# A decoder trunk in one program: the order of the attention's sigmoids, and where two pairs' products stand among the projections

## The chip, the cores and the metric

The kernel runs on one core of one Trainium2 chip. The metric is the device time of one execution in microseconds (us); below it is the median of three runs. A profile of one execution gives the start and the duration of every instruction on each engine: PE does the matmuls (PEld is its loading of weights), ACT and DVE the elementwise work, POOL small sums, and SP issues the transfers.

## The reference, cut to what matters

Two layers, each followed by a squared-ReLU MLP, over 512 tokens of width 1024. The first layer mixes by pooling, the second by stick-breaking attention with 16 heads of 64 channels. The change lies in the attention alone.

```python
def stick_breaking_attention(q, k, v):
    ...
    for i in range(S // Q_BLOCK):
        kv_len = (i + 1) * Q_BLOCK
        ...
        z = jnp.einsum('bhqd,bhkd->bhqk', q_blk, k_blk,
                       preferred_element_type=jnp.float32) * inv_sqrt_d
        ...
        log1m = jnp.where(mask, -jax.nn.softplus(z), 0.0)
        excl = lax.cumsum(log1m, axis=3, reverse=True) - log1m
        a = jnp.where(mask, jnp.exp(jax.nn.log_sigmoid(z) + excl), 0.0)
        outs.append(jnp.einsum('bhqk,bhkd->bhqd', a, v_blk.astype(jnp.float32)))
```

So a weight is sigmoid(z) times the product of the 1 - sigmoid(z) = sigmoid(-z) of all later keys before the query. The values are mixed with these weights, and the result goes through the output projection `w_o`.

## The kernel before, in words

Every fp32 operand of a matmul is split in two: a high half, cast by ACT (`nc.scalar.copy`), and the residual, subtracted by DVE. A product is then three matmuls: high by high, high by residual, residual by high. PSUM has eight tiles of 128x512, taken in turn as they come free (`ps()`).

The attention works on eight pairs of heads. `ATT_ORDER` is a written list of its steps, and PE's instructions stand in exactly that order; ACT, DVE and SP are ordered by a scheduler, except that ACT keeps the written order inside `weights`. A step is a letter, the pair, and digits:

- K: the first slices of a pair's key projection (`start`). A projection has eight slices of three matmuls of 128x512; K22 does two slices for pair 2.
- P: the rest of the key projection, then the query projection (`queries_keys`, `project`). ACT casts kh and qh (L967), DVE subtracts kl and ql (L968). Behind each of the two a `fill()` asks for the next weights.
- S: the scores of both heads (`scores`, L1084) into six PSUM tiles, three per head, then `weights`. ACT computes per head four negative sigmoids u (`against`, L1007, the factors 1 - sigmoid) and three positive ones w (`for_`, L1019). A PSUM tile of scores is free once its positive sigmoid is done. DVE runs a scan over u (L1023, tile e) and multiplies w by it (`weigh`, L1029). There is one e, so the second head's scan follows the first head's multiplication.
- T: PE transposes the w of both heads (`turn`, L1042) into six PSUM tiles; ACT casts ah (L1048) and DVE subtracts al (L1052), which frees the tile.
- A: the products of a pair with the values (`products`, L1059), one PSUM tile per head; ACT copies a half of it to o (L1066), DVE adds the other half (L1070). The pair's output o is split into two halves, both called ohl (ACT L292, DVE L293), which the output projection O reads (L311 to L313).

The steps of one pair are spread over three rounds: while S works on pair p, A works on pair p - 1. In the second and the third round a copy (ACT L170) and a residual (DVE L172) of a weight of the output projection are made as well.

Of the kernel before, what the change touches and what calls it, by code (L numbers as in the profile page):

```python
# [15 lines left out]
P = 128  # L16
# [41 lines left out]

ATT_ORDER = [
    (w[0], int(w[1]), [int(c) for c in w[2:]])  # L60
    for w in """H001 N2 H101 N3 H023 H123 P0 K12 S0 P1 T0 K22 S1 A0 P2 T1 K32 S2 A1 P3 O001 T2 O023 S3 A2 P4 V20 T3 V21
    S4 A3 P5 V22 T4 V23 S5 A4 P6 V30 T5 V31 S6 A5 V323 P7 T6 E1""".split()
]

# [41 lines left out]
def trunk(ctx, tc, x, consts, grow, pw, wup, wdn, wq, wk, wv, wo, out):  # L106
# [68 lines left out]
    def gains(lo, n):  # L175


        def scaled(raw):
            m = max(n, 4)
            for k in range(m):  # L180
                c, at = raw[:, k * D // m : (k + 1) * D // m], lo + k * n // m
                nc.scalar.mul(c, c, gc[:, at : at + 1])  # L182

        return scaled
# [3 lines left out]
    def want(key, src, scaled=None):  # L188
        queue.append((key, src, scaled))
# [57 lines left out]
    def fill(n=1):  # L247
        if gate[0]:
            behind.update(latest)
        for _ in range(n):  # L250
            if queue and len(made) < ahead and (queue[0][0][0] != "dn" or dn_pool[0]):
                make()
# [6 lines left out]
    for l in range(2):  # L259
        if l == 1:  # L260
            n = len(queue)
            for what, i, part in ATT_ORDER:
                if what == "H" and not i and 0 in part:
                    for h in range(4):
                        want(("v", 0, h), wv[h], gains(C_KV * KC + 2 * h, 2))
                elif what == "V" and 0 in part:
                    for h in range(2):
                        want(("v", i, h), wv[2 * i + h], gains(C_KV * KC + 4 * h, 4))
                elif what == "K":
                    want(("k", i), wk[i], gains(C_KV * KC, KC))  # L270
                elif what == "P":
                    if ("k", i) not in [k for k, _, _ in queue]:
                        want(("k", i), wk[i], gains(C_KV * KC, KC))
                    want(("q", i), wq[i], gains(C_MIX_PRE1 * KC, KC))
                elif what == "O" and 0 in part or what == "E":
                    for c in range(2 * i, 2 * i + 2 if what == "O" else PAIRS):
                        want(("o", c), wo[c])
            apart.extend(x for x in queue[n:] if x[0] not in [("o", c) for c in range(2)])
            at = [k for k, _, _ in apart].index(("v", 0, 2))
            later = [apart.pop(at) for _ in range(2)]  # L280
            at = [k for k, _, _ in apart].index(("q", 1)) + 1
            apart[at:at] = later

            queue[n - GRP : n + GRP] = queue[n : n + GRP] + queue[n - GRP : n]
        for j in range(NJ):
            want(("up", l, j), wup[l, j])
        for j in range(NJ - GRP, NJ):
            want(("dn", l, j), wdn[l, j])
# [153 lines left out]
    def need(*tiles):  # L442
        for t in tiles:
            if t in pending:
                pending.pop(t).transpose()
# [444 lines left out]
    with tc.tile_pool(name="att", bufs=1, reuse_waits="tile") as ap:  # L890
# [14 lines left out]
        def half_values(i, part):  # L905


            if not half_w:
                half_w.extend(get(("v", 0, h)) for h in range(4))
                for u in range(2):  # L910
                    vs[u] = None, value_tile(u)
            for s in part:
                if i == 0:
                    half_bank[s] = ps()
                for k in range(4 * i, 4 * i + 4):
                    (wh, wl), c = half_w[k // 2], NS[k % 2]
                    mm3(
                        half_bank[s], xnh[:, k, TS[s]], xnl[:, k, TS[s]], wh[:, c], wl[:, c], k == 0, k == KC - 1
                    )
                if i == 1:  # L920
                    for u in range(2):
                        value_parts(vs[u][1], s, half_bank[s][:, u * 256 : u * 256 + 256])
            if i == 1 and T - 1 in part:
                fill(ahead)

        def values(u, part):
            if u not in vs:
                vs[u] = [get(("v", u, h)) for h in range(2)], value_tile(u)
            w, v = vs[u]
            for s in part:  # L930
                pv = ps()
                for k in range(KC):
                    c = slice((k % 4) * 256, (k % 4) * 256 + 256)
                    mm3(
                        pv[:, :256], xnh[:, k, TS[s]], xnl[:, k, TS[s]],
                        w[k // 4][0][:, c], w[k // 4][1][:, c], k == 0, k == KC - 1,
                    )
                value_parts(v, s, pv[:, :256])
# [3 lines left out]
        def start(key, n):  # L942

            started[key] = ps(), get(key), n
            up_block(*started[key][:2], slice(0, S), ks=range(n))

        def project(key):
            if key in started:
                pq, w, n = started.pop(key)
                up_block(pq, w, slice(0, S), ks=range(n, KC))  # L950
            else:
                pq = ps()
                up_block(pq, get(key), slice(0, S))
            return pq

        def qk_tile(tag):
            return ap.tile([P, S], F32R, tag=tag, name=name(tag))
# [1 line left out]
        half = [slice(0, HD), slice(HD, P)]  # L959


        def queries_keys(p):
            both = []
            for what in "kq":
                src = project((what, p))
                hi, lo = qk_tile(f"{what}h"), qk_tile(f"{what}l")
                latest["act"] = nc.scalar.copy(hi, src)  # L967
                latest["dve"] = nc.vector.tensor_tensor(out=lo, in0=src, in1=hi.bitcast(F32), op=ALU.subtract)  # L968
                both.append((hi, lo))
                fill()  # L970
            return both

        begin = ap.tile([P, NSEG], mybir.dt.bfloat16, tag="begin", name="begin")
        us = [ap.tile([P, NSEG + 1], F32, tag=f"u{a}", name=f"u{a}") for a in range(2)]
# [97 lines left out]
        def scores(hs, b):  # L1072


            (kh, kl), (qh, ql) = hs[0].qk
            for x in hs:
                x.pz[b] = ps()
            o = 0
            for i in Head.SCORES[b][0]:
                n = SEG[i][1]  # L1080
                for m, (x, y) in enumerate(((qh, kh), (qh, kl), (ql, kh))):
                    for h in hs:
                        own = half[h.a]
                        nc.tensor.matmul(  # L1084
                            h.pz[b][:, o : o + n], x[own, TS[i]], y[own, :n], start=m == 0, stop=m == 2,
                        )
                o += n

        def weights(p):
            hs = [Head(qk[p], p, a) for a in range(2)]  # L1090
            for b in range(3):
                scores(hs, b)
            with tc.manual_schedule(engines={mybir.EngineType.Activation}):
                for x in hs:
                    for b in range(3):
                        x.against(b)
                hs[0].scan()
                for x in hs:
                    for b in range(3):
                        x.for_(b)  # L1100
            hs[0].weigh()
            hs[1].scan()
            hs[1].weigh()
            return hs

        def transposed(hs):
# [146 lines left out]
        def until(key):  # L1253
            while key not in made:
                make()

        qk, heads, gpost1 = {}, {}, None

        def step(what, i, part):
            nonlocal gpost1  # L1260
            if what == "H":
                half_values(i, part)
            elif what == "V":
                values(i, part)
            elif what == "N":
                need(i)
            elif what == "K":
                start(("k", i), *part)
            elif what == "P":
                qk[i] = queries_keys(i)  # L1270
                if i == PAIRS - 1:
                    until(("o", 5))
            elif what == "S":
                gate[0] = True
                heads[i] = weights(i)
                fill()
            elif what == "T":
                transposed([heads[i][a] for a in part or range(2)])
                behind.update(latest)
            elif what == "A":  # L1280
                mix_pair(i, vs[i // 2][1])
            elif what == "O" and part:
                out_proj(i, part)
                if gpost1 is None:
                    with tc.issue_after(latest["sp"].ins):
                        gpost1 = gain_row(R_MIX_POST1)
# [66 lines left out]
```

## Time and profile before

| | us |
|---|---|
| median of 3 runs | 950.59 (949.9 to 950.76) |
| profiled execution | 950.39 |
| its span | 948.6 |
| first to last step of interest: S1 to the first output projection | 419.50 to 455.16 |

A row of the page's busy times gives an engine's busy us, its share of the span and its instructions. A row of waits reads: engine, tile and line, then what it waited for, with us in total, times, and the longest. A row of windows gives a stretch in us from the span's start, its length, then the busy us of PE, PEld, DVE, ACT and POOL (with the count of instructions), the clock that PE was granted, the share of the transfer engines and GB/s. A row of the timeline gives the start, the duration, engine, line and operation, out<-in, and in brackets the idle time before it and who ended it; x6 means that six such instructions are drawn together.

### The profile page before, as it was taken

What the parts mean: (1) busy time and instruction counts of PE and PEld (TensorE: products, weight loads), DVE (VectorE), ACT (ScalarE), POOL (GpSimd) and SP (SyncE); (2) the same over time, 40 slices, a digit from 0 to 9 for tenths busy, and PEclk for the clock granted to TensorE, in tenths of its full rate; (3) what the DMA queues carried; (4) which work ended last, traced back from release to release, by engine and by line L of the source; (5) the groups of instructions that cost most, each with busy time, mean ns of one, the idle gap of its engine ahead of it and who ended that gap; (6) DMA issues with size and microseconds to landing.
All of it is one profiled execution on the core that took longest, in us unless ns stands there. A gap on an engine that the chain in (4) does not pass through costs nothing.

```text
span 948.6 us, 12348 instructions
## 1 busy us (share of the span) xinstructions
PE 937.6 (99%) x4702; PEld 789.9 (83%) x4702; DVE 696.4 (73%) x797; ACT 560.4 (59%) x983; POOL 41.1 (4%) x83
## 2 busy tenths in 40 slices
PE   9999999999999999999999999999999999999996
PEld 7998888888888888887888988898888888888885
DVE  5865798988978976178466668884696966958756
ACT  6667979788775646165544444875645444444532
POOL 2300000000000004000000000200000000000002
PEclk9999999999999999999999999999999999999999
DMA  8244969789697860630434271342514243133102
GB/s 309 95 181 140 348 218 346 293 284 353 216 326 264 298 195 2 222 133 1 170 119 171 97 267 45 134 156 74 193 45 133 89 133 111 45 133 112 37 7 90
DMA packets 43262, 156.15 MB, mean 165 GB/s; under 512 B 4289, under 2 KB 4673, under 8 KB 43202
## 3 DMA queue, kind: packets, MB, share of 16 engines
q1 hardware_dynamic: 43202, 155.36, 46.7%
q8 instruction: 37, 0.61, 0.3%
q14 instruction: 23, 0.19, 0.1%
HBM read 121.79 MB, written 33.55 MB: 164 GB/s over the span
## 4 chain that ended last, share of the span: by engine, by line
PE 96%; ACT 1%; DVE 1%; POOL 1%; issue 0%; POOLq 0%; DVEq 0%; ACTq 0%
PE ps L600 28%; PE ps L722 15%; PE ps L719 15%; PE ps L723 15%; PE ps L311 4%; PE ps L312 4%; PE ps L313 4%; PE ps L1059 2%; PE ps L1042 2%; PE ps L1084 2%; PE ps L840 1%; PE ps L406 1%; PE ps L812 1%; PE ps L767 1%; ACT xn L296 1%; ACT u L1007 0%
## 5 line engine op out<-in xcount | busy, mean ns | idle before, releaser
L600 PE MATMUL ps<-w,a 128*128 128x512 f32 x1176 | 278.6, 389 | 0.0
L722 PE MATMUL ps<-xnh,w 128*128 128x512 f32 (+1 forms) x704 | 260.2, 371 | 0.0
L723 PE MATMUL ps<-xnl,w 128*128 128x512 f32 (+1 forms) x704 | 259.7, 370 | 0.0
L719 PE MATMUL ps<-xnh,w 128*128 128x512 f32 (+1 forms) x704 | 259.1, 370 | 0.1
L600 PEld LDWEIGHTS ps<-w,a 128*128 128x128 f32 x1176 | 220.7, 188 | 45.9 <-DVE w L293 0.2
L719 PEld LDWEIGHTS ps<-xnh,w 128*128 128x128 f32 x704 | 132.1, 188 | 22.9 <-DVE w L861 0.3
L723 PEld LDWEIGHTS ps<-xnl,w 128*128 128x128 f32 x704 | 132.7, 188 | 22.1
L722 PEld LDWEIGHTS ps<-xnh,w 128*128 128x128 f32 x704 | 132.2, 188 | 22.3
L609 DVE TENSOR_TENSOR y<-ps,y 128x512 f32<-128x512 f32 x124 | 84.3, 686 | 43.8 <-PE ps L600 43.7
L172 DVE TENSOR_TENSOR w<-raw,w 128x1024 fp32r<-128x1024 f32 x58 | 70.9, 1222 | 57.2 <-ACT w L170 57.1
L170 ACT CAST w<-raw 128x1024 fp32r<-128x1024 f32 x58 | 61.0, 1051 | 80.3 <-PE ps L719 80.3
L292 ACT CAST a<-r 128x768 fp32r<-128x768 f32 (+1 forms) x60 | 47.6, 794 | 72.0 <-PE ps L600 55.4
L293 DVE TENSOR_TENSOR a<-r,a 128x768 fp32r<-128x768 f32 (+1 forms) x60 | 54.0, 900 | 11.8 <-ACT a L292 11.6
L1023 DVE TENSOR_TENSOR_SCAN e<-u,begin 128x1280 f32<-128x1280 f32 x16 | 45.2, 2825 | 18.6 <-ACT u L1007 18.3
L292 ACT CAST w<-e 128x1536 fp32r<-128x1536 f32 (+1 forms) x30 | 41.9, 1395 | 23.3 <-DVE e L574 13.9
L293 DVE TENSOR_TENSOR w<-e,w 128x1536 fp32r<-128x1536 f32 (+1 forms) x30 | 49.4, 1647 | 1.8 <-ACT w L292 1.6
L182 ACT ACTIVATE apart<-apart,eye 128x128 f32<-128x128 f32 (+1 forms) x132 | 43.1, 407 | 0.3 <-DMA apart<-in_wk 0.3
L293 DVE TENSOR_TENSOR w<-w,w 128x1536 fp32r<-128x1536 f32 (+1 forms) x20 | 33.0, 1649 | 8.4 <-ACT w L292 8.4
L632 ACT ACTIVATE r<-ps 128x512 f32<-128x512 f32 x56 | 33.0, 590 | 8.8 <-PE ps L719 8.7
L293 DVE TENSOR_TENSOR w<-xn,w 128x1536 fp32r<-128x1536 f32 (+1 forms) x20 | 33.0, 1650 | 5.6 <-ACT w L292 5.5
L633 ACT ACTIVATE r<-r 128x512 f32<-128x512 f32 x56 | 35.5, 634 | 1.3
L296 ACT ACTIVATE xn<-y 128x512 f32<-128x512 f32 (+1 forms) x25 | 15.3, 613 | 32.2 <-DVE y L478 28.6
(134 smaller groups left out, 1327.6 us busy)
## 6 DMA issues: line engine op xcount, KB each, us to landing
raw<-in_wup SPq DMA_DIRECT2D x64, 512.0 KB, 4.1
w<-kept SPq DMA_DIRECT2D x60, 512.0 KB, 4.3
kept<-wx SPq DMA_DIRECT2D x30, 512.0 KB, 4.7
w<-in_wdn SPq DMA_DIRECT2D x8, 1536.0 KB, 6.7
kept<-apart SPq DMA_DIRECT2D x24, 512.0 KB, 6.0
xn<-in_wdn SPq DMA_DIRECT2D x8, 1536.0 KB, 7.6
apart<-in_wk SPq DMA_DIRECT2D x7, 512.0 KB, 7.5
apart<-in_wq SPq DMA_DIRECT2D x7, 512.0 KB, 9.3
```

The costliest lines, as they stand in the source:

```text
L170: nc.scalar.copy(hi, raw)
L172: nc.vector.tensor_tensor(out=lo, in0=raw, in1=hi.bitcast(F32), op=ALU.subtract)
L182: nc.scalar.mul(c, c, gc[:, at : at + 1])
L292: latest["act"] = nc.scalar.copy(hi, src)
L293: latest["dve"] = nc.vector.tensor_tensor(out=lo, in0=src, in1=hi.bitcast(F32), op=ALU.subtract)
L311: nc.tensor.matmul(dst, ah, bh, start=start, stop=False)
L600: nc.tensor.matmul(bank, a[:, x, q, TS[t]], w[:, z, q], start=start and q == 0 and k == 0, stop=q == self.n - 1 and k == 2, skip_group_che ...
L609: nc.vector.tensor_tensor(out=part, in0=bank, in1=part, op=ALU.add)
L719: nc.tensor.matmul(pu[:, cols], wl[:, k, :], xnh[:, k, cols], start=False, stop=k == KC - 1)
L722: nc.tensor.matmul(pu[:, cols], wh[:, k, :], xnh[:, k, cols], start=k == 0, stop=False)
L723: nc.tensor.matmul(pu[:, cols], wh[:, k, :], xnl[:, k, cols], start=False, stop=False)
L1023: nc.vector.tensor_tensor_scan(out=self.e[:, ::-1], data0=self.u[:, 1:][:, ::-1], data1=begin[:, ::-1], initial=0.0, op0=ALU.mult, op1=ALU ...
```

## The change

`weights` computes the sigmoids of one head completely, negative and positive, followed by its scan and its multiplication, and then those of the other head. The pairs P2 and P3 are cut in two steps, J for the keys and Q for the queries, and the products of the pair before (A0, A1) stand between them instead of ahead of both. K2 and K3 start three slices instead of two.

```diff
 ATT_ORDER = [
-    for w in """H001 N2 H101 N3 H023 H123 P0 K12 S0 P1 T0 K22 S1 A0 P2 T1 K32 S2 A1 P3 O001 T2 O023 S3 A2 P4 V20 T3 V21
+    for w in """H001 N2 H101 N3 H023 H123 P0 K12 S0 P1 T0 K23 S1 J2 A0 Q2 T1 K33 S2 J3 A1 Q3 O001 T2 O023 S3 A2 P4 V20 T3 V21
...
-        def queries_keys(p):
-            both = []
-            for what in "kq":
+        def queries_keys(p, which="kq"):
+            for what in which:
...
-                both.append((hi, lo))
+                qk.setdefault(p, []).append((hi, lo))
                 fill()
-            return both
...
                 for x in hs:
                     for b in range(3):
                         x.against(b)
-                hs[0].scan()
-                for x in hs:
                     for b in range(3):
                         x.for_(b)
-            hs[0].weigh()
-            hs[1].scan()
-            hs[1].weigh()
+                    x.scan()
+                    x.weigh()
...
-            elif what == "P":
-                qk[i] = queries_keys(i)
+            elif what in "PJQ":
+                queries_keys(i, {"P": "kq", "J": "k", "Q": "q"}[what])
```

PE in the second round, at the end of the scores S1 (the tile ps431 holds the last scores, ps439 the first product, ps425 the keys of pair 2). Before:

```order
L1084 MATMUL ps431_3591<-kh401_3481,ql405_3511 128x128
L1059 MATMUL ps439_3635<-ah408_3518,v367_3176 128x512
L1059 MATMUL ps439_3635<-al409_3519,v367_3176 128x512
L1059 MATMUL ps439_3635<-ah411_3527,v367_3176 128x384
L1059 MATMUL ps439_3635<-al412_3528,v367_3176 128x384
```

Now:

```order
L1082 MATMUL ps431_3594<-kh401_3481,ql405_3511 128x128
L722 MATMUL ps425_3567<-xnh_80,w384_3363 128x512
L723 MATMUL ps425_3567<-xnl_81,w384_3363 128x512
L719 MATMUL ps425_3567<-xnh_80,w384_3363 128x512
L722 MATMUL ps425_3567<-xnh_80,w384_3363 128x512
```

The 16 matmuls of the products follow after 15 matmuls of the keys, and 24 of the queries come behind them; the third round is changed in the same way.

ACT in the same round (u1 is head 1's negative sigmoids, w433 and w432 head 0's positive ones, w434 head 1's, o the pair's output, ohl its high half, w436 a weight of the output projection, kh the keys of pair 2). Before:

```order
L1007 ACTIVATE u1_3146<-ps431_3591 128x127
L1019 ACTIVATE w433_3616<-ps426_3574 128x512
L1019 ACTIVATE w433_3616<-ps428_3582 128x384
L1019 ACTIVATE w433_3616<-ps430_3590 128x384
L1019 ACTIVATE w434_3620<-ps427_3575 128x512
L1019 ACTIVATE w434_3620<-ps429_3583 128x384
L1019 ACTIVATE w434_3620<-ps431_3591 128x384
L1066 COPY o438_3634<-ps439_3635 64x512
L1066 COPY o438_3634<-ps440_3646 64x512
L292 CAST ohl441_3657<-o438_3634 128x512
L170 CAST w436_3629<-raw437_3630 128x1024
L967 CAST kh442_3678<-ps425_3567 128x512
```

Now:

```order
L1005 ACTIVATE u1_3146<-ps427_3578 128x511
L1005 ACTIVATE u1_3146<-ps429_3586 128x383
L1005 ACTIVATE u1_3146<-ps431_3594 128x255
L1005 ACTIVATE u1_3146<-ps431_3594 128x127
L1017 ACTIVATE w434_3624<-ps427_3578 128x512
L1017 ACTIVATE w434_3624<-ps429_3586 128x384
L1017 ACTIVATE w434_3624<-ps431_3594 128x384
L170 CAST w436_3632<-raw437_3633 128x1024
L966 CAST kh438_3652<-ps425_3567 128x512
L1064 COPY o440_3656<-ps441_3657 64x512
L1064 COPY o440_3656<-ps442_3668 64x512
L292 CAST ohl443_3679<-o440_3656 128x512
```

Head 0's three positive sigmoids have moved ahead of head 1's negative ones, and the weight's copy and kh have moved ahead of the output's copies and its cast; behind the cast stand, as before it, the queries' cast, a second weight's copy and the six casts of the transposes.

DVE in the same round. Before:

```order
L1029 TENSOR_TENSOR w433_3616<-w433_3616,e432_3614 128x1280
L1023 SCALAR_TENSOR_TENSOR e435_3626<-u1_3146,begin_3144 128x1280
L1070 TENSOR_TENSOR o438_3634<-ps439_3635,o438_3634 64x512
L1070 TENSOR_TENSOR o438_3634<-ps440_3646,o438_3634 64x512
L1029 TENSOR_TENSOR w434_3620<-w434_3620,e435_3626 128x1280
L293 TENSOR_TENSOR ohl441_3657<-o438_3634,ohl441_3657 128x512
L172 TENSOR_TENSOR w436_3629<-raw437_3630,w436_3629 128x1024
L968 TENSOR_TENSOR kl443_3679<-ps425_3567,kh442_3678 128x512
L968 TENSOR_TENSOR ql446_3708<-ps444_3682,qh445_3707 128x512
L172 TENSOR_TENSOR w447_3711<-raw448_3712,w447_3711 128x1024
L1052 TENSOR_TENSOR al451_3718<-ps449_3716,ah450_3717 128x512
```

Now:

```order
L1027 TENSOR_TENSOR w432_3613<-w432_3613,e433_3617 128x1280
L1021 SCALAR_TENSOR_TENSOR e435_3628<-u1_3146,begin_3144 128x1280
L172 TENSOR_TENSOR w436_3632<-raw437_3633,w436_3632 128x1024
L1027 TENSOR_TENSOR w434_3624<-w434_3624,e435_3628 128x1280
L967 TENSOR_TENSOR kl439_3653<-ps425_3567,kh438_3652 128x512
L1068 TENSOR_TENSOR o440_3656<-ps441_3657,o440_3656 64x512
L1068 TENSOR_TENSOR o440_3656<-ps442_3668,o440_3656 64x512
L293 TENSOR_TENSOR ohl443_3679<-o440_3656,ohl443_3679 128x512
L967 TENSOR_TENSOR ql446_3708<-ps444_3682,qh445_3707 128x512
L172 TENSOR_TENSOR w447_3711<-raw448_3712,w447_3711 128x1024
L1050 TENSOR_TENSOR al451_3718<-ps449_3716,ah450_3717 128x512
```

The weight's residual and kl have moved ahead of the two adds of o, and the multiplication of head 1 stands ahead of them too; the residual of the output is the neighbour of ql now.

More of the change, by code (lines that the diff above doesn't have):

```diff
@@ L270, in trunk @@
                     want(("k", i), wk[i], gains(C_KV * KC, KC))
-                elif what == "P":
+                elif what in "PQ":
                     if ("k", i) not in [k for k, _, _ in queue]:
@@ L1268, in step @@
                 start(("k", i), *part)
-            elif what == "P":
-                qk[i] = queries_keys(i)
+            elif what in "PJQ":
+                queries_keys(i, {"P": "kq", "J": "k", "Q": "q"}[what])
                 if i == PAIRS - 1:
```

## The prediction

> **What bounds the kernel now.** I read the page first: its span, its busy times and the shares of the chain that ended last.
>
> ```profile
> span 948.6 us, 12348 instructions
> PE 937.6 (99%) x4702; PEld 789.9 (83%) x4702; DVE 696.4 (73%) x797; ACT 560.4 (59%) x983; POOL 41.1 (4%) x83
> PE 96%; ACT 1%; DVE 1%; POOL 1%; issue 0%; POOLq 0%; DVEq 0%; ACTq 0%
> ```
>
> PE sets the end. The change adds and removes no matmul, so only PE's waits can be won or lost. This execution took 950.39 us, 1.8 more than its span; the median of the three runs, 950.59, lies 0.20 above it. What a measurement of this kernel can tell from no change is about 0.2%, 1.9 us.
>
> The list of PE's waits comes next, and then the windows of PE's steps: the scores of S1, S2 and S3, the products of A0, A1 and A2, and the projections P2 and P3.
>
> ```profile
> PE ps L1059 <- ACT w L1019: 2.1, 2, 1.1
> PE ps L1084 <- DVE al L1052: 0.2, 1, 0.2
> ```
>
> ```profile
> 419.50:421.56 2.06, 2.06 (x25) 1.88 (x24) 0.90 (x2) 1.07 (x2) 0.00 (x0) 1.00 0.27 103
> 438.75:441.74 2.99, 2.77 (x26) 2.15 (x25) 2.43 (x5) 1.70 (x4) 0.00 (x0) 1.00 0.00 0
> 468.64:470.71 2.07, 2.07 (x26) 1.87 (x25) 0.00 (x0) 1.60 (x3) 0.00 (x0) 1.00 0.79 247
> 421.56:425.45 3.89, 2.81 (x18) 2.49 (x17) 3.04 (x2) 3.73 (x11) 0.00 (x0) 1.00 0.00 1
> 441.74:445.55 3.81, 2.84 (x18) 2.50 (x17) 3.06 (x2) 3.75 (x11) 0.00 (x0) 1.00 0.00 0
> 470.71:473.30 2.59, 2.59 (x19) 2.42 (x17) 1.84 (x1) 2.44 (x9) 0.00 (x0) 1.00 0.94 373
> 425.45:435.08 9.63, 9.63 (x45) 7.90 (x44) 9.19 (x8) 3.98 (x7) 0.00 (x0) 1.00 0.00 0
> 445.55:455.16 9.61, 9.61 (x44) 7.93 (x44) 8.03 (x7) 3.00 (x6) 0.00 (x0) 1.00 0.30 110
> ```
>
> The first figure of a row is the stretch. Products without a wait take 2.59 (A2), so A0 loses 1.30 and A1 1.22. Scores take 2.07 (S3), so S2 loses 0.92. That is 3.44 in all, and it bounds the gain here. P2 and P3 hold 42 matmuls each, 0.229 apiece. The granted clock is 1.00 everywhere.
>
> By the idle of the wait list the same three losses are 2.3. [...] With the idle alone the sum below would come to 1.3 instead of 1.8. I go by the stretches.
>
> ```profile
> 424.13 0.50 PE L1059 MATMUL ps<-ah,v 128*128 128x512 f32 x1 [1.08 <-ACT w L1019]
> 444.21 0.50 PE L1059 MATMUL ps<-ah,v 128*128 128x512 f32 x1 [0.97 <-ACT w L1019]
> 440.90 0.38 PE L1084 MATMUL ps<-kh,qh 64*128 64x256 f32 x1 [0.22 <-DVE al L1052]
> 438.42 0.40 PE L719 MATMUL ps<-xnh,w 128*128 128x512 f32 x1
> 438.75 0.53 PE L1084 MATMUL ps<-kh,qh 64*128 64x512 f32 x2
> ```
>
> The kernel has eight PSUM banks. In A0 and A1 six hold scores, one the half-done key projection, one the first head's product; the second product (424.13, 444.21) waits until ACT's first positive sigmoid frees a score bank. In S2 the scores wait for banks that DVE's residuals (al) of the transposes free.
>
> ```profile
> 420.49 1.07 ACT L1007 ACTIVATE u<-ps 128x511 f32<-128x511 f32 x2 [1.36 <-PE ps L1084]
> 421.72 1.87 ACT L1007 ACTIVATE u<-ps 128x255 f32<-128x255 f32 x6 [0.16 <-PE ps L1084]
> 423.42 2.68 ACT L1019 ACTIVATE w<-ps 128x512 f32<-128x512 f32 x6
> 426.13 1.19 ACT L1066 COPY o<-ps 64x512 f32<-64x512 f32 x2
> 430.90 0.62 ACT L292 CAST ohl<-o 128x512 fp32r<-128x512 f32 x1 [3.59 <-DVE o L1070]
> 431.43 1.05 ACT L170 CAST w<-raw 128x1024 fp32r<-128x1024 f32 x1
> 432.50 0.59 ACT L967 CAST kh<-ps 128x512 fp32r<-128x512 f32 x1
> 435.33 0.59 ACT L967 CAST qh<-ps 128x512 fp32r<-128x512 f32 x1 [2.24 <-PE ps L719]
> 435.81 1.05 ACT L170 CAST w<-raw 128x1024 fp32r<-128x1024 f32 x1
> 436.76 2.60 ACT L1048 CAST ah<-ps 128x512 fp32r<-128x512 f32 x6
> ```
>
> ```profile
> 422.31 2.82 DVE L1023 TENSOR_TENSOR_SCAN e<-u,begin 128x1280 f32<-128x1280 f32 x1 [1.91 <-ACT u L1007]
> 425.23 1.49 DVE L1029 TENSOR_TENSOR w<-w,e 128x1280 f32<-128x1280 f32 x1
> 426.76 2.82 DVE L1023 TENSOR_TENSOR_SCAN e<-u,begin 128x1280 f32<-128x1280 f32 x1
> 429.50 1.37 DVE L1070 TENSOR_TENSOR o<-ps,o 64x512 f32<-64x512 f32 x2
> 430.90 1.49 DVE L1029 TENSOR_TENSOR w<-w,e 128x1280 f32<-128x1280 f32 x1
> 432.31 0.68 DVE L293 TENSOR_TENSOR ohl<-o,ohl 128x512 fp32r<-128x512 f32 x1
> 432.91 1.22 DVE L172 TENSOR_TENSOR w<-raw,w 128x1024 fp32r<-128x1024 f32 x1
> 434.05 0.68 DVE L968 TENSOR_TENSOR kl<-ps,kh 128x512 fp32r<-128x512 f32 x1
> 435.95 0.69 DVE L968 TENSOR_TENSOR ql<-ps,qh 128x512 fp32r<-128x512 f32 x1 [1.22 <-ACT qh L967]
> 436.90 1.23 DVE L172 TENSOR_TENSOR w<-raw,w 128x1024 fp32r<-128x1024 f32 x1 [0.25 <-ACT w L170]
> 438.04 3.14 DVE L1052 TENSOR_TENSOR al<-ps,ah 128x512 fp32r<-128x512 f32 x6
> ```
>
> These are ACT's and DVE's queues for the second step. From 422.31 to the end of the residuals at 441.18 DVE stands still for some 1.5 us only; this chain decides when S2 gets its banks.
>
> **The sigmoids, head by head.** The same 14 per pair, in another order. The first positive one now follows head 0's four negative ones, which end just before the scan at 422.31; from its start to the product that it frees are 424.13 - 423.42 = 0.71. With nothing else changed the bank would be free at about 423.0, and the second product asks for it at 421.56 + 1.30 = 422.86: the wait would be nearly gone by this alone. The two parts of the change cure the same wait and do not add. Head 1's negative sigmoids come three positive ones later (2.68 / 6 = 0.45 each, 1.35), ready at 421.72 + 1.87 + 1.35 = 424.9, before the second scan at 426.76; that slack of 1.8 is the cover, beyond it each us would be a us of DVE's chain. The other pairs showed no such wait, so I cost the order there at nothing.
>
> **The products moved.** K2 and K3 start three slices of eight instead of two: 3 x 0.229 = 0.69 ahead of S1 and S2, and as much less behind. Then come the other 15 key matmuls (3.43), the products, 24 query matmuls (5.49). PE's clock in step 2:
> S1 starts at 419.50 + 0.69 = 420.19 and ends at 422.25; keys to 425.68; one more switch between kinds of matmul, 438.75 - 438.42 = 0.33 instead of 0.23, so 0.10; products 2.59 without wait to 428.37 (the second asks at about 427.1, its bank is free near 423.7); queries to 433.86. That is 1.22 before the old 435.08. The fills of weights, two per pair, keep their order on SP, and PE's list names no wait for a DMA; cost nothing.
>
> **What is late next: the banks of S2.** The transposes and the first slices took 435.08 to 438.75, 3.67; with the third slice 4.36, so PE asks for S2 at 433.86 + 4.36 = 438.22, 0.53 earlier than before. DVE's chain begins 0.69 later and has another order: the second scan at 427.45; the weight residual 430.19; the second weighing 431.33; kl 432.74; both adds of o from 433.34 to 434.71 (steps between starts as in the rows: 2.74, 1.14, 1.41, 0.60, 1.37). ACT's cast ohl waits for these adds: 434.74 to 435.36; behind it qh to 435.9 and the weight copy to about 436.9; DVE's weight residual then, and al at 436.93 + 1.14 = 438.07, against 438.04. So S2's banks come when they came, S2 ends at 441.74 again, and its wait grows from 0.92 to 441.74 - 438.22 - 2.07 = 1.45. PE's gain of step 2 goes over into this wait, but for the slice of 0.69 that now lies ahead of it.
>
> **Behind S2.** Keys 3.43, switch 0.10, products 2.59 and queries 5.49 end at 453.35; before, 455.16. The output projection needs the pair's second ohl three matmuls in (454.0) and its residual five in (454.5). By the chain above from S2's end (scan 0.75 behind it, as 422.31 to 421.56; then 4.45, 2.74, 0.60, 0.70, 1.41, 0.70) the cast ends at about 453.7, the residual at 454.4: just in time.
>
> The sum: 1.30 + 1.22 won in the products, 0.53 given back in S2, twice 0.10 in switches: 1.79, or 455.16 - 453.35 = 1.81. The profiled execution would take 948.6, and the median 950.59 - 1.8 = **948.8**. Bounds of the terms: the switch costs nothing to 0.2 each; DVE's idle in the new chain (about 0.9) may vanish, which gives 0.9 more, or al may come late; the second ohl, with 0.1 to 0.3 to spare, may cost 0.4. I take the middle ones, since each step has its row. The case's own range is 948.3 to 949.3.
>
> **Rivals.**
> S2's wait shrinks too: al comes 0.9 earlier, since the weight copies ahead of it need nothing late. The gain is 2.7, the time 947.9; with no wait in S2 at all 1.45 + 1.81 = 3.26 and 947.3. For it: T1 starts 1.2 earlier. Against it: ohl, qh and the copy must still follow the adds.
> Everything goes into S2: al and the second ohl come about 1.2 later than I reckon, and some 0.5 of gain is left, 950.1. Nothing in the rows asks for so much.
> ACT's queue stops: slower. The cast ohl waits for DVE's adds, and now qh, a weight copy and all six ah stand behind it, where only a copy and kh stood before. In the old rows kh was cast at 432.50 though its 18 matmuls had ended at 425.45 + 18 x 0.229 = 429.6: the queue did stop behind ohl. If nothing overlapped behind the weighing, kl, adds, ohl, its residual, qh, ql, copy and residual would add up to 0.68 + 1.37 + 0.62 + 0.68 + 0.59 + 0.69 + 1.05 + 1.22 = 6.9, and al would start at 432.74 + 6.9 = 439.6, 1.6 late. Paid in S2 and again before the output projection that is 3.2 against 1.8: 952.0. It decides once the two delays pass 1.8 together, and shows as slower past 3.7.
> The Trainium skill (PSUM — Partial Sum Buffer, Engine vs sequencer instructions) says that ScalarE's and VectorE's queues are strictly first in, first out, which is the rule behind this rival; the trace agrees with the 2.9 between 429.6 and 432.50.
>
> **How the numbers follow.** Forecast 0.60; less wait in S2 0.22; all into S2 0.08; the stopped queue 0.10. The line of 0.2% is 948.69, inside the forecast's own range: I give 0.27 of its 0.60 to faster and 0.33 to the same. The first rival is faster (0.22), the second the same (0.08), the third 0.07 slower and 0.03 the same. Faster 0.49, same 0.44, slower 0.07. The range reaches over most of the first rival and short of the stopped queue: 947.5 to 950.1.
>
> **What would show it.** Right: no wait of the products on the positive sigmoid; S2's stretch near 3.5; al starting with the same distance to S2's end; products at 2.6; the output projection some 1.8 earlier, and the rest shifted by that. Wrong: S2's stretch near 2.1 to 2.6 (first rival) or over 4, a wait of the output projection for ohl, or of the second scan for head 1's sigmoids.

## The result, and the profile after

| | before | after |
|---|---|---|
| median of 20 runs | 950.55 us | 948.63 us |
| span of the profiled execution | 948.6 us | 946.7 us |
| K2's first slice to the output projection O001 | 37.23 us | 35.50 us |
| the 24 matmuls of O001 | 5.61 us | 5.70 us |

The ratio is 0.998, 95% interval 0.9973 to 0.9987: faster by 0.2%. The interval lies wholly below 1, and the 1.92 us are about the 1.9 that the prediction took as the least that can be told from no change.

From the page of the changed kernel: span, busy times, and the chain that ended last.

```profile
span 946.7 us, 12348 instructions
PE 937.5 (99%) x4701; PEld 789.6 (83%) x4702; DVE 696.2 (74%) x797; ACT 560.0 (59%) x983; POOL 41.1 (4%) x83
PE 95%; DVE 2%; ACT 1%; POOL 1%; issue 1%; POOLq 0%; DVEq 0%; ACTq 0%
```

PE's busy time is what it was; only waits went. PE's list of waits now names, of the attention, only this:

```profile
PE ps L1082 <- DVE al L1050: 0.4, 2, 0.2
```

The products no longer stand there. How much that is worth the windows tell (us of the stretch first). Two stretches of before that were not shown yet, from the first slice of K2 to O001, and O001's first 24 matmuls:

```profile
417.93:455.16 37.23, 34.96 (x199) 29.00 (x198) 30.76 (x31) 21.85 (x48) 0.00 (x0) 1.00 0.14 51
...
455.16:460.77 5.61, 5.61 (x26) 4.47 (x25) 0.69 (x1) 2.35 (x4) 0.00 (x0) 1.00 0.54 187
```

The same work in the changed kernel as a whole, and then J2, A0, Q2, S2, A1 and O001:

```profile
417.75:453.25 35.50, 35.09 (x199) 29.06 (x198) 29.97 (x30) 21.25 (x48) 0.00 (x0) 1.00 0.15 54
...
422.11:425.64 3.53, 3.53 (x17) 2.92 (x16) 2.81 (x1) 3.39 (x10) 0.00 (x0) 1.00 0.00 0
425.64:428.13 2.49, 2.49 (x17) 2.32 (x16) 2.28 (x3) 2.47 (x6) 0.00 (x0) 1.00 0.00 0
428.13:433.67 5.54, 5.54 (x26) 4.51 (x26) 5.54 (x5) 1.11 (x2) 0.00 (x0) 1.00 0.00 0
438.04:441.69 3.65, 3.24 (x26) 2.27 (x25) 3.09 (x7) 2.36 (x6) 0.00 (x0) 1.00 0.00 0
...
445.22:447.71 2.49, 2.49 (x17) 2.32 (x16) 2.34 (x2) 1.98 (x5) 0.00 (x0) 1.00 0.52 156
...
453.25:458.95 5.70, 5.70 (x25) 4.39 (x24) 1.30 (x2) 2.72 (x5) 0.00 (x0) 1.00 0.52 185
```

Products that took 3.89 and 3.81 take 2.49 each. S2 took 2.99 and takes 3.65. Over the stretch 37.23 - 35.50 = 1.73 is won, and 0.09 of it is lost again inside O001. The span shows 1.9, but the trace of after is 0.18 ahead of the other already at S0, the first pair's scores (403.92 against 404.10), ahead of which no instruction has moved, and still so where K2 starts (417.75 against 417.93); that part is not the change's, and its cause stays open. In the ten kernels of the experiments K2 starts anywhere from 417.60 to 418.11.

ACT's and then DVE's timeline of the changed kernel, from the first pair's cast ohl to the residuals al of the transposes:

```profile
434.64 0.62 ACT L292 CAST ohl<-o 128x512 fp32r<-128x512 f32 x1 [5.38 <-DVE o L1068]
435.28 0.58 ACT L966 CAST qh<-ps 128x512 fp32r<-128x512 f32 x1
435.76 1.05 ACT L170 CAST w<-raw 128x1024 fp32r<-128x1024 f32 x1
436.71 2.60 ACT L1046 CAST ah<-ps 128x512 fp32r<-128x512 f32 x6
```

```profile
433.22 1.39 DVE L1068 TENSOR_TENSOR o<-ps,o 64x512 f32<-64x512 f32 x2
435.29 0.69 DVE L293 TENSOR_TENSOR ohl<-o,ohl 128x512 fp32r<-128x512 f32 x1 [0.69 <-ACT ohl L292]
435.90 0.69 DVE L967 TENSOR_TENSOR ql<-ps,qh 128x512 fp32r<-128x512 f32 x1
436.85 1.23 DVE L172 TENSOR_TENSOR w<-raw,w 128x1024 fp32r<-128x1024 f32 x1 [0.26 <-ACT w L170]
437.99 3.14 DVE L1050 TENSOR_TENSOR al<-ps,ah 128x512 fp32r<-128x512 f32 x6
```

The queries' matmuls end at 433.67, but qh is cast at 435.28: ACT stands idle for 5.38 ahead of ohl, which waits for DVE's adds of o, and the last 0.97 of this (433.67 to 434.64) and ohl itself lie behind the end of the queries. From the end of the queries to al it was 438.04 - 435.08 = 2.96 before and is 437.99 - 433.67 = 4.32 now. From al's start to the end of S2 it is 3.70 in both (441.74 - 438.04, 441.69 - 437.99).

### The profile page after: what moved, and what is told of

Same layout as the page of the kernel before. It is cut to its first block, busy times and chain, and to the rows that moved or that the text cites. A ratio compares the mean times of both kernels' runs of the same rounds, so it can differ in the third digit from the quotient of the medians.

```text
span 946.7 us, 12348 instructions
## 1 busy us (share of the span) xinstructions
PE 937.5 (99%) x4701; PEld 789.6 (83%) x4702; DVE 696.2 (74%) x797; ACT 560.0 (59%) x983; POOL 41.1 (4%) x83
## 4 chain that ended last, share of the span: by engine, by line
PE 95%; DVE 2%; ACT 1%; POOL 1%; issue 1%; POOLq 0%; DVEq 0%; ACTq 0%
PE ps L600 28%; PE ps L722 15%; PE ps L719 15%; PE ps L723 15%; PE ps L312 4%; PE ps L311 4%; PE ps L313 4%; PE ps L1057 2%; PE ps L1082 2%; PE ps L1040 2%; PE ps L840 1%; PE ps L406 1%; PE ps L812 1%; PE ps L767 1%; ACT xn L296 1%
```

## The experiments

Each kernel has its own before on the same chip (medians 950.42 for e1 to e4, 950.34 for e5 to e8, 950.63 for e9 and e10). The columns, worked out from each kernel's timeline, are: K2's first slice to O001; from the end of the queries to al; S2; al to the end of S2; O001's 24 matmuls; the median; the ratio to before with its interval.

| | K2 to O001 | to al | S2 | al to S2's end | O001 | median | ratio |
|---|---|---|---|---|---|---|---|
| before | 37.23 | 2.96 | 2.99 | 3.70 | 5.61 | 950.55 | |
| after | 35.50 | 4.32 | 3.65 | 3.70 | 5.70 | 948.63 | 0.998 (0.9973 to 0.9987) |
| e1 sigmoids alone | 34.71 | 2.96 | 2.98 | 3.69 | 5.60 | 947.64 | 0.9972 (0.9961 to 0.9984) |
| e2 move alone | 35.39 | 4.24 | 3.58 | 3.70 | 5.65 | 948.63 | 0.9982 (0.9973 to 0.9991) |
| e3 two slices | 35.44 | 3.67 | 3.68 | 3.68 | 5.60 | 948.42 | 0.9978 (0.997 to 0.9987) |
| e4 sigmoids, three slices | 34.46 | 3.32 | 2.65 | 3.69 | 5.60 | 947.63 | 0.9971 (0.996 to 0.9983) |
| e5 late residual | 33.99 | 2.84 | 2.16 | 3.69 | 5.71 | 947.34 | 0.9968 (0.9955 to 0.998) |
| e6 late ohl | 34.09 | 2.91 | 2.23 | 3.69 | 5.70 | 947.34 | 0.9969 (0.9957 to 0.9981) |
| e7 fourth slice | 34.80 | 4.33 | 2.98 | 3.70 | 6.40 | 948.84 | 0.9984 (0.9975 to 0.9992) |
| e8 sigmoids, late residual | 33.80 | 1.54 | 2.05 | 4.18 | 5.60 | 946.97 | 0.9964 (0.9951 to 0.9976) |
| e9 sigmoids, K33 | 34.03 | 2.96 | 2.29 | 3.69 | 5.61 | 946.87 | 0.9962 (0.9949 to 0.9974) |
| e10 sigmoids, K34 | 33.80 | 2.97 | 2.06 | 4.14 | 5.85 | 947.25 | 0.9964 (0.9951 to 0.9978) |

### The parts apart: e1 to e4

**e1**, the new `weights` with the old steps:

```diff
-K23 S1 J2 A0 Q2 T1 K33 S2 J3 A1 Q3 O001
+K22 S1 A0 P2 T1 K32 S2 A1 P3 O001
```

> Only the new order of the sigmoids; the steps stand as before (K22, A0 ahead of P2, A1 ahead of P3). Theory (either part cures the products' wait by itself; the rest is decided by when al frees S2's banks): no wait of the products for a positive sigmoid, A0 and A1 at about 2.6 each instead of 3.89 and 3.81; the adds of o stay ahead of the weighing, so al comes about 1.2 earlier with the products and S2's wait stays near 0.9 or falls; output projection about 2.4 earlier than before, that is more than the whole change won (1.9), median near 948.1. Rival (the gain is the move's: another step must stand between scores and products): products keep waits of 0.5 or more each, output projection at most 1.2 earlier, median 949.3 or above.

The windows of e1 (the whole stretch, A0, S2, A1) and its rows of qh and al:

```profile
417.83:452.54 34.71, 34.49 (x200) 28.89 (x198) 30.67 (x31) 21.96 (x48) 0.00 (x0) 1.00 0.15 54
421.47:424.08 2.61, 2.61 (x19) 2.44 (x17) 1.87 (x1) 2.46 (x7) 0.00 (x0) 1.00 0.00 2
437.35:440.33 2.98, 2.76 (x25) 2.12 (x24) 2.43 (x5) 1.71 (x4) 0.00 (x0) 1.00 0.00 0
440.33:442.94 2.61, 2.61 (x18) 2.44 (x17) 1.96 (x1) 2.54 (x8) 0.00 (x0) 1.00 0.00 0
```

```profile
433.94 0.59 ACT L966 CAST qh<-ps 128x512 fp32r<-128x512 f32 x1 [2.43 <-PE ps L719]
```

```profile
436.64 3.14 DVE L1050 TENSOR_TENSOR al<-ps,ah 128x512 fp32r<-128x512 f32 x6
```

Products at 2.61 without a wait, and S2's wait no longer than before: 37.23 - 34.71 = 2.52, the two products' 1.30 and 1.22 in full. qh is cast 0.26 after its matmuls (433.68), behind an ohl that was done at 431.50. The new order of the sigmoids alone wins more than the whole change: five of its six runs lie below the fastest of the twenty of after (947.97).

**e2**, the steps of the change with the old `weights`:

```diff
                 for x in hs:
                     for b in range(3):
                         x.against(b)
+                hs[0].scan()
+                for x in hs:
                     for b in range(3):
                         x.for_(b)
-                    x.scan()
-                    x.weigh()
+            hs[0].weigh()
+            hs[1].scan()
+            hs[1].weigh()
```

> Only the moved products and the third slices; the sigmoids in the old order. Theory: products at 2.6 without a wait too, S2's stretch about 3.7 as in the changed kernel, output projection about 1.8 earlier than before, median near 948.8: the same as the whole change, so the sigmoids' order adds nothing to it. Rival (each part is worth a share, the shares add up to the 1.9): output projection about 1 earlier, median near 949.6, with a wait of products or of the scores' banks that the changed kernel lacks.

The windows of A0 and S2 in e2:

```profile
425.49:427.97 2.48, 2.48 (x17) 2.31 (x16) 2.34 (x3) 2.46 (x6) 0.00 (x0) 1.00 0.00 0
437.88:441.46 3.58, 3.24 (x25) 2.27 (x25) 3.02 (x6) 2.29 (x5) 0.00 (x0) 1.00 0.00 0
```

The move alone gives the whole change's time, 948.63, with the same long S2. Either part cures the products' wait; once the move is made, the sigmoids' order adds nothing that can be measured.

**e3**, K22 and K32 in the changed kernel, the rest as it is:

```diff
-K23 S1 J2 A0 Q2 T1 K33 S2 J3 A1 Q3 O001
+K22 S1 J2 A0 Q2 T1 K32 S2 J3 A1 Q3 O001
```

> The changed kernel with two slices of K2 and K3 instead of three. Theory (S2's banks come when DVE's chain lets them; a slice ahead of S2 only fills that wait, but S1 then starts 0.69 earlier and DVE's chain with it): al 0.7 earlier against the changed kernel, S2's stretch about as long as with three slices (3.6), output projection within 0.2 of the changed kernel's, median near 948.6. Rival (the third slice is what hides S2's wait): S2's stretch 0.7 longer than in the changed kernel, output projection 0.7 later, median 949.3.

S2's window in e3:

```profile
437.19:440.87 3.68, 3.22 (x25) 2.25 (x24) 3.14 (x7) 2.41 (x6) 0.00 (x0) 1.00 0.00 0
```

S2 is as long as with three slices, and O001 is reached as soon (35.44 against 35.50). A slice ahead of both S1 and S2 moves DVE's chain as much as PE, and wins nothing: the third slices of the change are idle.

**e4**, the sigmoids and the third slices, without the move:

```diff
-K23 S1 J2 A0 Q2 T1 K33 S2 J3 A1 Q3 O001
+K23 S1 A0 P2 T1 K33 S2 A1 P3 O001
```

> The new order of the sigmoids and the third slices, but the products ahead of both projections as before. Theory (with the products early, DVE's adds of o and ACT's cast ohl come early as well, the chain to al has its old order and the third slice covers what is left of S2's wait): S2 at about 2.1 to 2.3, products 2.6, output projection about 2.9 earlier than before, median near 947.7, 1.0 better than the changed kernel: the move then costs 1.0. Rival (the move takes work off DVE's chain ahead of S2): S2 at 3.5 or more, output projection no earlier than in the changed kernel, median 948.6 or above.

S2's window in e4, and the first residual al:

```profile
438.38:441.03 2.65, 2.44 (x25) 2.04 (x24) 2.10 (x5) 1.01 (x2) 0.00 (x0) 1.00 0.00 0
```

```profile
437.34 0.69 DVE L1050 TENSOR_TENSOR al<-ps,ah 128x512 fp32r<-128x512 f32 x1
```

Half a miss. It is better than the changed kernel by 1.04 over the stretch, as expected, but S2 takes 2.65, not 2.1 to 2.3. S1 starts 0.69 later with three slices, so the scans and al come later too (3.32 behind the queries instead of 2.96), and that eats half of the slice. The median, 947.63, is e1's.

### What holds S2: e5 and e6

**e5** puts the second output weight's cast and residual, which stood between ql and al, behind the transposes':

```diff
+    put_off = []
...
+        if k == ("o", 1):
+            raw = wts.tile([P, D], F32, tag="raw", bufs=2, name=name("raw"))
+            nc.sync.dma_start(raw, src)
+            hi, lo = made[k] = place(k)
+            def halves():
+                with tc.issue_after(latest["act"].ins):
+                    nc.scalar.copy(hi, raw)
+                with tc.issue_after(latest["dve"].ins):
+                    nc.vector.tensor_tensor(out=lo, in0=raw, in1=hi.bitcast(F32), op=ALU.subtract)
+            put_off.append(halves)
+            return
...
             elif what == "T":
                 transposed([heads[i][a] for a in part or range(2)])
+                if put_off:
+                    put_off.pop()()
```

> The changed kernel, but the cast and the residual of the second output-projection weight (ACT and DVE, 1.05 and 1.23 between ql and al) are issued behind the casts and residuals of the second step's transposes; its transfer stays where it was. Theory (DVE's chain alone holds S2's banks): al starts right behind ql, about 1.4 earlier (436.6 instead of 437.99); S2 takes 2.1 to 2.3 instead of 3.65; the output projection comes about 1.4 earlier; the weight's residual fits between al and the next scan; median near 947.2. Rival (S2 waits for something else, such as ACT's casts or the order of the banks): S2 stays above 3.2 and the median above 948.2.

DVE's rows in e5 (the added lines shift the numbers: L982 is ql, L1065 al, L256 the weight's residual), and the window of S2:

```profile
436.09 0.69 DVE L982 TENSOR_TENSOR ql<-ps,qh 128x512 fp32r<-128x512 f32 x1
436.70 3.14 DVE L1065 TENSOR_TENSOR al<-ps,ah 128x512 fp32r<-128x512 f32 x6
439.75 1.22 DVE L256 TENSOR_TENSOR w<-raw,w 128x1024 fp32r<-128x1024 f32 x1
```

```profile
438.23:440.39 2.16, 2.16 (x25) 1.97 (x24) 2.16 (x5) 2.16 (x5) 0.00 (x0) 1.00 0.00 0
```

al follows ql at once, S2 falls from 3.65 to 2.16, and 35.50 - 33.99 = 1.51 is won. The residual of 1.22 lies behind al, where DVE had nothing to do. S2 waited for DVE's chain.

**e6** leaves that weight alone and puts the first pair's ohl, cast and residual, behind the transposes':

```diff
+    put_off = []
...
-            split(o, *os[p])
+            if p:
+                split(o, *os[p])
+            else:
+                put_off.append((o, os[p]))
...
                 transposed([heads[i][a] for a in part or range(2)])
+                if put_off:
+                    o, both = put_off.pop()
+                    with tc.issue_after(latest["act"].ins):
+                        latest["act"] = nc.scalar.copy(both[0], o)
+                    with tc.issue_after(latest["dve"].ins):
+                        latest["dve"] = nc.vector.tensor_tensor(
+                            out=both[1], in0=o, in1=both[0].bitcast(F32), op=ALU.subtract
+                        )
```

> The changed kernel, but ACT's cast ohl of the first pair and its residual are issued behind the casts and residuals of the second step's transposes; nothing needs them before the output projection. Theory (what the move costs is that ohl, which waits for the late adds of o, stands ahead of qh and the weight copy in ACT's queue): qh starts about 1.2 earlier, at the end of its matmuls (434.0 instead of 435.28), al 1.2 to 1.4 earlier, S2 at 2.2 to 2.5, the output projection 1.2 to 1.4 earlier, median near 947.3. Rival (al is late through DVE's own work, the two scans and the residuals, and not through ACT's queue): al at most 0.6 earlier, S2 above 3, median above 948.0.

ACT's rows in e6, then DVE's al, then the window of S2:

```profile
433.80 0.59 ACT L968 CAST qh<-ps 128x512 fp32r<-128x512 f32 x1 [4.63 <-PE ps L721]
434.28 1.05 ACT L170 CAST w<-raw 128x1024 fp32r<-128x1024 f32 x1
```

```profile
436.51 3.14 DVE L1052 TENSOR_TENSOR al<-ps,ah 128x512 fp32r<-128x512 f32 x6
```

```profile
437.97:440.20 2.23, 2.23 (x25) 1.97 (x25) 2.23 (x5) 1.39 (x3) 0.00 (x0) 1.00 0.00 0
```

qh is cast 0.20 after the queries (433.60) and not 1.61; al comes 2.91 behind them and not 4.32; S2 takes 2.23. What the move costs is this cast with its residual: the products come later, the adds of o with them, and ohl, which nobody needs yet, holds up qh, the weight and al. The run moves both, so it does not say how the 1.41 divides between the cast in ACT's queue (0.62) and the residual in DVE's (0.69).

### What binds behind S2: e7

```diff
-T1 K33 S2
+T1 K34 S2
```

> The changed kernel with K34 instead of K33: one more slice (0.69) ahead of S2, one less behind it. Theory (al does not move, S2 ends when it ended, and the second ohl, whose chain starts at S2's end, binds next): S2 asks 0.69 later and takes 2.9 to 3.0; the output projection is reached 0.7 earlier, but waits there for ohl and its residual, 0.6 to 0.8 more in all (its 24 matmuls take 6.3 to 6.5 instead of 5.70); median 948.5 to 948.7, no gain. Rival (S2's wait is the only loss left): the output projection's 24 matmuls keep 5.6 to 5.7, median 947.9.

S2 and O001 in the windows of e7, and PE's row in O001 that waited:

```profile
438.68:441.66 2.98, 2.76 (x26) 2.11 (x25) 2.42 (x5) 1.68 (x4) 0.00 (x0) 1.00 0.00 0
452.51:458.91 6.40, 6.13 (x26) 4.32 (x24) 1.73 (x3) 2.97 (x5) 0.00 (x0) 1.00 0.44 165
```

```profile
453.65 0.50 PE L311 MATMUL ps<-w,ohl 128*128 128x512 f32 x1 [0.27 <-ACT ohl L292]
```

S2 waits 0.67 less, O001 takes 0.70 more: the same 41.20 in both kernels. The second pair's ohl is the next bound, as the chain behind S2's end had it.

### Versions with the sigmoids alone: e8 to e10

**e8** is e5 with the old steps, so e1 with e5's late residual:

```diff
-K23 S1 J2 A0 Q2 T1 K33 S2 J3 A1 Q3 O001
+K22 S1 A0 P2 T1 K32 S2 A1 P3 O001
```

> The sigmoids alone (steps as before, e1) with the second weight's cast and residual behind the transposes' as in e5. Theory: al starts 1.2 to 1.4 earlier than in e1 (436.64), S2 falls from 2.98 to 2.1, the output projection comes 0.9 earlier than in e1, no wait is left in the second and the third step; median near 946.8, the best of all. Rival (the wait of S2 in e1 has another cause): S2 above 2.7 and the median as e1's, 947.6.

The windows of e8, the whole stretch and S2:

```profile
417.82:451.62 33.80, 33.80 (x200) 28.66 (x198) 30.57 (x31) 21.89 (x48) 0.00 (x0) 1.00 0.15 56
437.34:439.39 2.05, 2.05 (x25) 1.87 (x24) 2.05 (x4) 1.62 (x3) 0.00 (x0) 1.00 0.00 0
```

PE is busy through the whole stretch, and S2 is as short as a free one.

**e9** and **e10** are e1 with one and two slices more, ahead of S2 only (K33 and K34):

```diff
-K22 S1 A0 P2 T1 K32 S2 A1 P3 O001
+K22 S1 A0 P2 T1 K33 S2 A1 P3 O001
```

> The sigmoids alone (e1) with one slice more ahead of S2 only (K22 and K33). Theory (al stands where it stood, 436.64, since nothing ahead of it moves; the slice fills S2's wait): S2's stretch falls by 0.7 from 2.98 to 2.3, the output projection 0.7 earlier than in e1 (452.54), and the second ohl still comes in time; median near 946.9. Rival (S2's end is not set by al but moves with PE's own work): S2 keeps 2.98 and the output projection e1's time, median 947.6.

> As e9 with K34, two slices more ahead of S2 (1.38, where 0.91 are waited). Theory: S2 without a wait at 2.1, the output projection 0.9 earlier than in e1, no more than in e8; median near 946.8. Rival (each slice is worth 0.69): the output projection 1.4 earlier than in e1, median 946.3.

The window of S2 in e9:

```profile
437.90:440.19 2.29, 2.29 (x26) 1.97 (x25) 1.74 (x4) 1.02 (x2) 0.00 (x0) 1.00 0.00 0
```

And S2 and O001 in e10, with O001's sixth matmul, the one behind it, and DVE's residual of the second pair's ohl:

```profile
438.93:440.99 2.06, 2.06 (x26) 1.85 (x25) 1.06 (x3) 1.00 (x2) 0.00 (x0) 1.00 0.00 0
451.84:457.69 5.85, 5.85 (x26) 4.39 (x24) 1.86 (x4) 2.36 (x4) 0.00 (x0) 1.00 0.52 181
```

```profile
453.15 0.50 PE L313 MATMUL ps<-w,ohl 128*128 128x512 f32 x1
453.49 0.40 PE L311 MATMUL ps<-w,ohl 128*128 128x512 f32 x1
452.41 0.68 DVE L293 TENSOR_TENSOR ohl<-o,ohl 128x512 fp32r<-128x512 f32 x1
```

In e9 al stands where it stood in e1, and the slice goes into the wait in full: S2 falls from 2.98 to 2.29. In e10 the next slice wins 0.23 in the stretch and loses 0.24 in O001, so my number for its median, 946.8, was too low; I had left out that ohl comes due there too: the sixth matmul starts at 453.15, just behind the end of the residual at 453.09. To the end of O001 e9 and e10 take the same, 34.03 + 5.61 and 33.80 + 5.85, so the 0.38 between their medians of five runs does not come from this stretch. e9 needs one digit and the new `weights`, and with e8 it is the fastest of all: 946.87 and 946.97, against 948.63 of the changed kernel. Which of the two is better can't be told: e8 is 0.24 ahead to the end of O001, and e9 by its median.

## Why the prediction was right

The forecast was 948.8, with 948.3 to 949.3 for its own range; the median is 948.63, and the mechanism is the one predicted. With 0.18 added to the times of after, for the shift that lies ahead of the change:

- **The products.** Forecast: both waits vanish, 1.30 + 1.22. They did. A0 takes 2.49 where 2.59 was set; the keys and the queries around it take 0.15 more than their matmuls, which is the next point.
- **The extra switch.** Forecast 0.10 a step. J2, A0 and Q2 take 3.53 + 2.49 + 5.54 = 11.56 where 3.43 + 2.59 + 5.49 = 11.51 without it: 0.05, half the price.
- **PE's clock in step 2.** The queries were to end at 433.86; they end at 433.67 + 0.18 = 433.85.
- **S2.** al was to start at 438.07 and starts at 438.17; S2's wait was to grow from 0.92 to 1.45, and is 3.65 - 2.07 = 1.58. The chain was right in each link; its adds ended 0.07 later than reckoned.
- **Behind S2.** O001 at 453.35 was forecast; 453.43 came. The second ohl was to be cast by 453.7 and its residual done at 454.4; it was 453.80 and 454.53, and what was called just in time costs 0.10 in O001 (5.70 against 5.60 in e1). The forecast had nothing for it, and 0.4 as its bound. A wait of the output projection for ohl was also one of its signs of being wrong: it came, but too small to upset the sum.
- **The sum.** 1.81 at the start of O001 was forecast and 1.73 came, 1.64 behind it. The median fell by 1.92, which is 0.28 more than this; in the profiled pair 0.18 lies ahead of the change, and 0.09 behind O001 is not explained. So it is luck, in part, that the median came as near as 0.17 to the forecast; the stretches are what bears the mechanism out.

The three rivals fell. S2's wait did not shrink, and not everything went into it. The stopped queue exists: al is 4.32 behind the queries instead of 2.96, and e6 shows that ohl with its residual does it. But this stop was already in the forecast's chain; overlapped with DVE's own work it comes to 1.4 once, and to 0.10 at O001, not to 1.6 twice. The trace agrees with the Trainium skill's rule that ScalarE's queue is strictly first in, first out (PSUM — Partial Sum Buffer, Engine vs sequencer instructions): for the last 0.97 of the 5.38 that ACT idles ahead of ohl, the matmuls of qh are done, and qh stays behind ohl.

What the prediction left out: it said that either part cures the wait and that they don't add (e1 and e2 show it), and then priced only both together. By its own steps the sigmoids alone were worth 1.30 + 1.22 = 2.52, because without the move the adds and ohl stay early and al comes forward with PE. The step "PE's gain of step 2 goes over into this wait" is true of the moved order only, and e6 undoes it by moving one cast and its residual.

One rule covers S2 in all twelve kernels: it ends 3.7 after al starts (3.68 to 3.70 in the table), or 2.06 after PE asks (2.05 and 2.06), whichever is later. In before, after, e1 to e7 and e9 the first holds, in e8 and e10 the second.

## What to carry to other kernels

When two edits cure the same wait, price each alone against both together: the second may only bring its side effects. In an in-order queue, put a cast whose result is needed late behind those that others wait for, above all when its own input has just been made later. Filler work hides a wait only if it stands behind the start of the chain that ends the wait; in front of it it delays both.

## What the runs showed of the hardware that was not expected

The list of PE's waits shows far less than is lost. In the changed kernel it gives S2 0.4, while its stretch is 1.58 above a free one; in e9 and e5 S2 is 0.23 and 0.10 above 2.06 and the list names no wait of scores at all, and neither does it name O001's 0.25 in e10. Nor is the busy time of the windows a measure of it: S2's row before counts 2.77 as busy, where 2.07 do in S3. A matmul that waits a little can be drawn longer instead: the row of PE in the changed kernel's O001 that starts just behind the end of ohl's residual (454.35) reads 0.49, its neighbours 0.39 and 0.40.

```profile
454.18 0.40 PE L312 MATMUL ps<-w,ohl 128*128 128x512 f32 x1
454.42 0.49 PE L313 MATMUL ps<-w,ohl 128*128 128x512 f32 x1
454.75 0.39 PE L311 MATMUL ps<-w,ohl 128*128 128x512 f32 x1
```

A late start also hides in the overlap of the rows: one that is drawn 0.40 is followed 0.23 or 0.24 later by the next. In e10 the sixth matmul of O001 starts 0.37 behind the fifth, and the seventh 0.34 behind it, so 0.25 is lost and no idle is shown.

By the idle in the list the gain would have been put at 1.3; by the stretches it was put at 1.81, and 1.73 came. The list's total falls by 1.9, from 2.3 to 0.4, but this nearness is luck: it misses 0.4 to 0.5 of the products' losses before, and 0.7 of S2's before and 1.2 after.
